# A two-layer encoder step in fp32: a third raw weight buffer in the second layer, and the third row tile loaded early into a query slot

## The chip, the cores and the metric

The kernel runs on one core of a Trainium2 chip. The time is the device time of one execution in microseconds, and lower is better. The median of several executions of the whole program counts.

## The reference

The reference is one inference step of a small encoder with two layers. There are 1024 prompt rows (one stream) and 128 sample rows (8 running streams with 16 new rows each), all of width 1024. Everything is float32.

```python
for layer in range(2):
    if layer == 0:    # mixer A: own q, k, v; window of 2 earlier chunks; ALiBi; sinks
        q, k, v = project_a(h, g_attn[0], w_qkv_a[0], g_q_a[0], g_k_a[0])
    else:             # mixer B: shared k, v from h; own q; 8 earlier chunks; learned bias
        k, v = shared_kv(h, g_kv, w_kv, g_k_b)
        q = project_q_b(h, g_attn[1], w_q_b[0], g_q_b[0])
    h = h + attention(q, k, v) @ w_o        # 16 heads of 64, 4 key/value heads, chunks of 64
    h = h + square(relu(rmsnorm(h, g_mlp[layer]) @ w_up[layer])) @ w_down[layer]   # 1024 -> 4096 -> 1024
```

Each `project` is an RMS norm over the 1024 columns, a matrix product, and an RMS norm of each head's 64 numbers for queries and keys. The sample rows also attend to cached keys and values. The outputs are the final rows of both kinds and the new keys and values of both mixers.

## The kernel before

**Tiles.** The prompt is cut into eight row tiles of 128 rows, numbered 0 to 7; the sample rows are one more tile, `ST`, number 8. A row tile of x (128 × 1024 numbers) is 512 KB. Between the phases the tiles live in DRAM, one tensor `xd[t]` for each.

**Exact products from three passes.** TensorE works on rounded float32. So each operand is split into a high part (the rounded number) and a low part (the rest), and a product is three matmuls, high × high, high × low and low × high: lines L198 to L200 for the projections, L157 to L159 for the output projection, L727 to L729 for the MLP. The high and low parts of a transposed x tile are called `hh` and `hl`.

**Weights.** A block of weights is loaded by SyncE into a raw buffer (`raw`, 512 KB for each load, from the pool `self.rawp`) and then split into its place in `w`. In the second layer GpSimd makes the high part (L166) and VectorE the low part (L171); each reads the raw buffer, which is free for another load when both have read it. `load_block` (L127) loads four such pieces for the keys and values (w_kv) and four for each half of the query weights (w_q_b). `load_wo` (L140) loads eight pieces of the output weights. The pool has two buffers, and the tag `raw` is also used for other things of the same size: an x tile in front of its transposes (`X`, L1331), the stacked sample keys `kt8` (L1401), the residual tile `xo` of an output projection inside the attention phase (L1510), and some x tiles of the output projection's last phase (L638).

**Phases.** Each layer runs `attention`, `wo_phase` (the rest of the output projection and the norm before the MLP), `mlp_up` and `mlp_down`. There are pools for each phase. Memory of a finished phase is taken again by the next, so that a new tile may have to wait until an old one at the same place has been read or stored. The program is recorded in an order written by hand, and a scheduler with a cost model then sets the order on each engine; each engine runs its instructions strictly in that order, and SyncE issues nearly all loads and stores in one such sequence.

**The second layer's attention.** First come the weights of keys and values and the tiles x0, x1 and `ST`. Then follow, for each tile, these steps:

- `X(t)`: loads `xd[t]`. Tile `ST` goes into a buffer of `biasB`; the others go into a `raw` buffer.
- `N(t)`: transposes x on TensorE (L191), splits the result into `hh` (ScalarE, L109) and `hl` (VectorE, L115), and takes the statistics of the norm (ScalarE, `junk`, L182). `spill` stores `hh` and `hl` to `hTd[t]` (L1361) for later, since two halves of the queries are made from them at different times.
- `K1(t)`, `K2(t)`: projection of keys and values, then norm and transposes into `KT`.
- `Q1(t, nb)`, `Q2(t, nb)`: projection of one half of the queries (8 heads), then norm, and transposes (L241) into a tile `qT`, of which the pool `apool` has two buffers.
- `R(t)`: loads `hh` and `hl` back from `hTd[t]` (L1374) for the second half of the queries. `hh` and `hl` have one buffer each.
- the scores (L412, L480), the softmax and its products, and the output projection of finished tiles (`WO`, with `xo` and a store to `xd`).

The text order at the place of the change, with `A` false, is: `load_block` of keys and values, X(0), X(1), X(ST), N(0), N(1), N(ST), small loads, the first half of the query weights, K1 and K2 and Q1 of tiles 0, 1 and ST, X(2), Q2(0), N(2), X(3), and so on.

**The last phase of the output projection.** `wo_phase` fetches nine tiles of x, apart from those kept in memory, into five places in turn: two of tag `raw` and three of its own pool `work` (L637 to L640).

Of the kernel before, what the change touches and what calls it, by code (L numbers as in the profile page):

```python
# [16 lines left out]
P = 128  # L17
# [58 lines left out]
class Build:  # L76
# [40 lines left out]
    def raw(self, shape):  # L117
        self.nraw += 1
        pool, tag = self.raws[self.nraw % len(self.raws)]
        return pool.tile(shape, F32, tag=tag, name=tag, bufs=2)  # L120

    def load_block(self, dst, w, n0, g, ks=range(0, KC, 2), act=False):
        nc = self.nc
# [500 lines left out]
    def wo_phase(self, layer, sx, x8, wo):  # L624
        nc = self.nc
        with ExitStack() as st:
            self.psum_pools(st, f"wo{layer}", dict(m=(4, 1), g=(3, 1)), dict(m="m", n="g"))
            work = self.pool(st, f"wow{layer}")
            small = self.pool(st, f"wosm{layer}", 2)
            osp, xs = {}, {}  # L630
            lo, hi = slice(0, 512), slice(512, 1024)

            def O(t, z):
                if t in self.kept:
                    xs[t] = self.kept[t]
                    return
                if len(xs) % 5 < 2:  # L637
                    xs[t] = self.rawp.tile([P, D], F32, tag="raw", name="x")  # L638
                else:
                    xs[t] = work.tile([P, D], F32, tag="x", name="x", bufs=3)  # L640
                nc.sync.dma_start(xs[t], self.xd[t])
                if t in self.wo_done:
                    return
                with self.tc.high_priority(WO_PRIO) if len(osp) < 2 else nullcontext():
                    load_o(t, z)

            def second():
                self.last = work.tile([P, 4, P], F32, tag="o2", name="o2")
                return self.last

            def load_o(t, z):
                o = work.tile([P, 4, P], F32, tag=f"o{z}", name="o")
                self.load_halves(layer, 1, t, o, second, nc.vector)
                oh = work.tile([P, 4, P], F32R, tag=f"oh{z}", name="oh")
                ol = work.tile([P, 4, P], F32R, tag=f"ol{z}", name="ol")
                self.split(oh, ol, o)
                osp[t] = oh, ol

            def M(t):
                x = xs[t]  # L660
                for n in range(2) if t not in self.wo_done else ():
                    nn = slice(n * 512, n * 512 + 512)
                    ps = self.psum("m", [P, 512], "ps_wo")
                    self.wo_proj(ps, *osp[t], wo, nn)
                    nc.vector.tensor_tensor(x[:, nn], ps, x[:, nn], ALU.add)
                if t not in self.wo_done:
                    nc.scalar.dma_start(self.xd[t], x)
                if t not in self.kept:
                    self.norm(small, work.tile([P, D], mybir.dt.bfloat16, tag="junk", name="junk"), x)

            def turn(src, dst, c, d):
                ps = self.psum("n", [P, 4, P], "ps_n")
                for k in range(4):
                    nc.tensor.transpose(ps[:, k, :], src[:, k * P : (k + 1) * P], self.ident)
                self.split(dst[0][:, d, c], dst[1][:, d, c], ps)

            def S(i):
                x1, x2 = xs[i], xs[i + NT // 2]
                s = self.sums() if i else self.sums0
                tt = nc.gpsimd.tensor_tensor  # L680
                tt(s[0], x2[:, lo], x2[:, hi], ALU.add)
                tt(s[1], s[0], x1[:, lo], ALU.subtract)
                tt(s[2], x1[:, lo], x2[:, lo], ALU.subtract)
                tt(s[3], x1[:, hi], s[1], ALU.subtract)
                return [x1[:, lo], x1[:, hi], x2[:, hi], *s]

            def T(i, src):
                c = slice(i * P, i * P + P)
                for p in (0, 1, 2, 3, 4, 5, 6):
                    turn(src[p], sx[p], c, slice(0, 4))  # L690

            order = WO_ORDER[layer]
            ready, pend = set(), []
            z = 0
            for t in order[:2]:
                O(t, z % 2)
                z += t not in self.wo_done
            for n, t in enumerate(order):
                if n + 2 < NTILE:
                    O(order[n + 2], z % 2)  # L700
                    z += order[n + 2] not in self.wo_done
                M(t)
                ready.add(t)
                for f in pend:
                    f()
                pend = []
                if t == ST:
                    def sample():
                        for h in range(2):
                            turn(xs[ST][:, h * 512 : h * 512 + 512], x8, slice(0, P), slice(4 * h, 4 * h + 4))  # L710
                    pend.append(sample)
                elif (t + 4) % NT in ready:
                    i = t % 4
                    T(i, S(i))
            for f in pend:
                f()
# [451 lines left out]
    def run(self):  # L1168
# [9 lines left out]
        with ExitStack() as top:  # L1178
# [49 lines left out]
            for layer in range(2):  # L1228
                with ExitStack() as st:
                    low = st.enter_context(ExitStack())  # L1230
                    self.rawp = self.pool(low, f"raw{layer}", 2)
                    self.wa = [self.pool(low, f"wa{layer}")]
                    self.nw = 0
                    keep = self.pool(low, f"keep{layer}")
# [39 lines left out]
    def attention(self, layer):  # L1274
# [18 lines left out]
        with ExitStack() as st:  # L1293
# [28 lines left out]
            def X(t):  # L1322
                if A:
                    xr[t] = work.tile([P, D], F32, tag="x", name="x", bufs=2)
                elif t == ST:
                    nb = cfg["bias_bufs"]
                    x = ring.tile([P, G, 256], F32, tag="biasB", name="x", bufs=nb)
                    xr[t] = x.rearrange("p g k -> p (g k)")
                else:
                    xr[t] = self.rawp.tile([P, D], F32, tag="raw", name="x")  # L1330
                nc.sync.dma_start(xr[t], x_src(t))  # L1331
# [218 lines left out]
                self.load_block(wkv, wkv_src, kv0, gkv, [4, 6])  # L1550
                N(ST, "p")
            else:
                if 0 in psp:
                    X(0)
                if 0 in psp:
                    for k0 in range(0, KC, 2):
                        self.load_split(wkv, 0, [k0, k0 + 1])
                        if k0 == 2:
                            X(1)
                else:  # L1560
                    self.load_block(wkv, wkv_src, kv0, gkv)
                    X(0)
                    X(1)
                X(ST)
                N(0)
                N(1, "pt")
                if not cfg["late"]:
# [43 lines left out]
            spill(ST)  # L1611
            run(Q1(ST, 0, "s"))
            K2(ST)
            X(2)
            Q2(0, 0)
            N(2)
            X(3)
# [118 lines left out]
def make_plan(tail, second):  # L1736
    plan = {}
    for s in range(2 * NT):
        if s + 2 < NT:
            plan[2 * s] = [("Q", s + 2)]  # L1740
        elif s + 2 < 2 * NT:
            plan[2 * s] = [("R", second[s + 2 - NT])]
        if s + 3 < NT:
            plan[2 * s + 1] = [("K", s + 3)]
    plan[13] = [("R", ST)]
    plan.update(tail)
    return plan
# [7 lines left out]
WO_ORDER = [[0, 4, 1, 5, 2, 6, 7, 3, ST], [0, 4, 1, 5, 6, 2, 7, 3, ST]]  # L1755

CFG = [
    dict(banks=dict(g=(5, 1), s=(2, 1), m=(1, 1)), q_bufs=4, order={}, second=SECOND[0], plan=make_plan({15: [('A', 0)], 17: [('A', 1)], 19: [('A', 2)], 21: [('A', 3)], 23: [('A', 4)], 25: [('A', 5)], 30: [('A', 7)], 31: [('A', 6)], 32: [('A', 8), ('B', 0), ('B', 4), ('B', 7)]}, SECOND[0]),
        la=3, prio=0, xt={('A', 8): 'x', ('B', 7): 'x', ('B', 0): 'keep', ('B', 4): 'keep'}, late=0, eng='cgu', k2=3, q2=9, lead=3, sf=0, up=(99, 2, 0, 3), ld=((9, 9, 10, 10), (11, 11, 12, 13), (26, 27, 28, 29)), n='g', q='g', qrb=1, np=3, bias_bufs=3, p_bufs=3, psp=(), wr='mmmm', wt=(0, 0, 2, 0, 2, 2, 0, 0, 2), rx=1, kd=1, o2=0, sb=0),
    dict(banks=dict(g=(4, 1), s=(3, 1), m=(1, 1)), q_bufs=4, order={}, second=SECOND[1], plan=make_plan({15: [('A', 0)], 17: [('A', 1)], 19: [('A', 2)], 21: [('A', 3)], 23: [('A', 4)], 25: [('A', 5)], 27: [('A', 8)], 28: [('A', 7)], 29: [('A', 6)], 31: [('B', 0), ('B', 4), ('B', 1)], 32: [('B', 5), ('B', 2), ('B', 3)]}, SECOND[1]),  # L1760
        la=2, prio=1000, xt={('B', 0): 'keep', ('B', 4): 'keep', ('B', 1): 'hh', ('B', 5): 'hl', ('B', 2): 'hh', ('B', 3): 'hl'}, late=0, eng='Ogu', k2=3, q2=6, lead=9, sf=0, up=(4, 2, 0, 99), ld=((11, 11, 11, 11), (11, 11, 11, 11), (26, 27, 28, 29)), n='g', q='g', qrb=2, np=2, bias_bufs=2, p_bufs=10, psp=(), wr='mmmm', wt=(0, 0, 0, 1, 1, 1, 1, 1, 2), rx=0, kd=1, o2=1, sb=3),
]

# [43 lines left out]
```

## Time and profile before

| | us |
|---|---|
| median of 3 runs | 2391.8 |
| lowest, highest | 2388.46, 2393.51 |
| the profiled execution | 2387.86 |
| its span | 2386.1 |

The profile is that of a single execution, whose time, 2387.86 us, is its span and 1.76 us around it. Its mean granted TensorE clock is 0.996 of full speed. Lines such as L191 are lines of the kernel before. PE is TensorE (PEld its weight loads), DVE VectorE, ACT ScalarE, POOL GpSimd, SP SyncE.

The second layer's attention begins at about 1140 us, where the first layer's MLP ends, and its output projection ends at about 1680 us.

### The profile page before, as it was taken

How to read it: one execution, taken by the hardware profiler on the slowest of the kernel's cores; microseconds unless marked ns; L12 is line 12 of the kernel's file. 1: busy time of each engine (PE TensorE's matmuls, PEld its weight loads, DVE VectorE, ACT ScalarE, POOL GpSimd, SP SyncE). 2: the span in 40 equal slices, each digit the busy share in tenths (PEclk: the TensorE clock that was granted, in tenths of full speed). 3: DMA queues.
4: the chain of work that ended last, by engine and by line, in shares of the span. 5: the costliest groups of instructions: out<-in, count | busy, mean ns of one | idle time of the engine just before them, and what ended most of it. 6: DMA issues, size and time to landing. Idle time of an engine off the chain costs nothing.

```text
span 2386.1 us, 33438 instructions
## 1 busy us (share of the span) xinstructions
PE 2313.9 (97%) x11621; PEld 1931.7 (81%) x11621; DVE 1627.6 (68%) x3002; ACT 1216.5 (51%) x2423; POOL 540.8 (23%) x828
## 2 busy tenths in 40 slices
PE   7998999899999999999999999998999999999999
PEld 6787877788888878888778788887888888888887
DVE  6788786655565776776577876877555565777674
ACT  3777674555555432332267666665555555323321
POOL 4334332311221100000333444444111211000000
PEclk9999999999999999999999999999999999999999
DMA  7335545343443964333653655554443445734332
GB/s 258 119 108 169 170 146 200 129 146 126 157 146 123 356 213 149 119 128 109 232 153 112 198 166 167 168 168 169 142 142 129 158 145 203 274 133 159 117 113 115
DMA packets 217529, 383.78 MB, mean 161 GB/s; under 512 B 50248, under 2 KB 124944, under 8 KB 210192
## 3 DMA queue, kind: packets, MB, share of 16 engines
q1 hardware_dynamic: 194288, 305.08, 38.9%
q0 software_dynamic: 21776, 71.84, 7.8%
q10 hardware_dynamic: 1296, 4.72, 0.5%
q8 instruction: 92, 1.51, 0.3%
q14 instruction: 77, 0.63, 0.1%
HBM read 245.42 MB, written 135.09 MB: 159 GB/s over the span
## 4 chain that ended last, share of the span: by engine, by line
PE 79%; DVE 7%; DMA 7%; ACT 3%; issue 2%; POOL 1%; SPq 1%; ACTq 0%; DVEq 0%; POOLq 0%
PE ps_x L727 9%; PE ps_x L729 9%; PE ps_x L728 9%; PE ps_y L729 7%; PE ps_y L728 7%; PE ps_y L727 7%; PE ps_mm L198 3%; PE ps_mm L200 3%; PE ps_mm L199 3%; PE ps_tr L305 2%; PE ps_mm L157 1%; PE ps_mm L158 1%; PE ps_mm L159 1%; PE ps_s L729 1%; PE ps_s L728 1%
## 5 line engine op out<-in xcount | busy, mean ns | idle before, releaser
L109 ACT CAST w<-r 128x2048 fp32r<-128x2048 f32 x56 | 107.1, 1913 | 325.2 <-PE ps_y L729 213.0
L727 PE MATMUL ps_x<-w,s 128*128 128x512 f32 x512 | 199.6, 390 | 4.2 <-DVE hc L866 2.1
L729 PE MATMUL ps_x<-w,s 128*128 128x512 f32 x512 | 199.4, 389 | 0.0
L728 PE MATMUL ps_x<-w,s 128*128 128x512 f32 x512 | 199.3, 389 | 0.0
L198 PE MATMUL ps_mm<-w,hh 128*128 128x512 f32 x432 | 172.5, 401 | 7.3 <-POOL w L166 3.2
L200 PE MATMUL ps_mm<-w,hl 128*128 128x512 f32 x432 | 172.1, 399 | 1.6 <-DVE hl L115 0.8
L199 PE MATMUL ps_mm<-w,hh 128*128 128x512 f32 x432 | 170.9, 397 | 1.3 <-DVE w L171 1.1
L109 ACT CAST s<-s 128x2048 fp32r<-128x2048 f32 x56 | 107.1, 1913 | 118.1 <-DMA s<-hd 109.3
L115 DVE TENSOR_TENSOR w<-r,w 128x2048 fp32r<-128x2048 f32 x56 | 128.2, 2290 | 51.0 <-ACT w L109 51.0
L727 PE MATMUL ps_x<-sx,w 128*128 128x512 f32 (+1 forms) x408 | 157.9, 387 | 3.9 <-ACT hc L846 3.0
L1033 DVE TENSOR_TENSOR x<-ps_y,x 128x512 f32<-128x512 f32 x136 | 92.4, 687 | 100.8 <-PE ps_y L729 100.8
L729 PE MATMUL ps_x<-sx,w 128*128 128x512 f32 (+1 forms) x408 | 154.2, 378 | 0.0
L728 PE MATMUL ps_x<-sx,w 128*128 128x512 f32 (+1 forms) x408 | 154.1, 378 | 0.0
L109 ACT CAST w<-ru 128x512 fp32r<-128x512 f32 (+1 forms) x160 | 110.0, 708 | 85.5 <-PE ps_y L728 32.0
L729 PE MATMUL ps_y<-w,s 128*128 128x512 f32 x384 | 149.5, 389 | 0.0
L727 PE MATMUL ps_y<-w,s 128*128 128x512 f32 x384 | 149.4, 389 | 0.0
L728 PE MATMUL ps_y<-w,s 128*128 128x512 f32 x384 | 149.4, 389 | 0.0
L115 DVE TENSOR_TENSOR s<-s 128x2048 fp32r<-128x2048 f32 x56 | 128.0, 2286 | 29.1 <-ACT s L109 28.9
L115 DVE TENSOR_TENSOR ptl<-ps_tr,pth 128x512 fp32r<-128x512 f32 x180 | 122.5, 685 | 24.1 <-ACT pth L109 17.8
L115 DVE TENSOR_TENSOR w<-ru,w 128x512 fp32r<-128x512 f32 (+1 forms) x160 | 126.5, 793 | 11.2 <-ACT w L109 11.1
L115 DVE TENSOR_TENSOR wq<-ru,wq 128x1024 fp32r<-128x1024 f32 x32 | 39.7, 1240 | 131.9 <-ACT wq L109 131.9
L109 ACT CAST pth<-ps_tr 128x512 fp32r<-128x512 f32 x180 | 104.9, 595 | 45.0 <-PE ps_tr L305 36.7
(280 smaller groups left out, 6579.7 us busy)
## 6 DMA issues: line engine op xcount, KB each, us to landing
s<-hd SPq DMA_DIRECT2D x56, 1024.0 KB, 4.7
ru<-in_w_up SPq DMA_DIRECT2D x64, 512.0 KB, 4.0
r<-in_w_down SPq DMA_DIRECT2D x32, 1024.0 KB, 5.8
hd<-hc POOLq DMA_DIRECT2D x128, 256.0 KB, 2.7
hd<-hs POOLq DMA_DIRECT2D x96, 256.0 KB, 2.5
x<-xd SPq DMA_DIRECT2D x41, 512.0 KB, 4.4
o<-oTd SPq DMA_DIRECT2D x52, 256.0 KB, 5.0
xd<-xo SPq DMA_DIRECT2D x18, 512.0 KB, 2.8
```

Of the source, the lines that this page charges most:

```text
L109: a = nc.scalar.copy(hi, src)
L115: return a, e.tensor_tensor(lo, src, hi.bitcast(F32), ALU.subtract)
L157: nc.tensor.matmul(ps, oh[:, k, :], w[:, 0, k, nn], start=(k == 0), stop=False)
L158: nc.tensor.matmul(ps, oh[:, k, :], w[:, 1, k, nn], start=False, stop=False)
L198: nc.tensor.matmul(ps, a, w[:, 0, k, :], start=(k == 0), stop=False)
L199: nc.tensor.matmul(ps, a, w[:, 1, k, :], start=False, stop=False)
L200: self.lp = nc.tensor.matmul(ps, b, w[:, 0, k, :], start=False, stop=(k == KC - 1))
L305: self.lp = nc.tensor.transpose(pt[:, i, :], get(i), self.ident)
L727: a = mm(ps, ah, bh, start=first, stop=False, skip_group_check=True)
L728: mm(ps, ah, bl, start=False, stop=False, skip_group_check=True)
L729: return a, mm(ps, al, bh, start=False, stop=last, skip_group_check=True)
L1033: tt(xs[t][:, N[n]], ps, xs[t][:, N[n]], ALU.add)
```

## The change

The raw pool has as many buffers as a new entry of the layer's settings says: `rb=2` for the first layer, as before, and `rb=3` for the second. In `wo_phase` of the second layer the five places are now three of tag `raw` and two of `work`. In the attention of the second layer X(2) moves from behind K2(ST) to behind X(ST), and its tile is a `qT` buffer of `apool` instead of a `raw` buffer. Branches on `psp`, which is empty for both layers, are removed at that place. In the built program the scheduler sets the order of all this; on SyncE X(2) then comes right after X(1).

```diff
     def raw(self, shape):
         self.nraw += 1
         pool, tag = self.raws[self.nraw % len(self.raws)]
-        return pool.tile(shape, F32, tag=tag, name=tag, bufs=2)
+        return pool.tile(shape, F32, tag=tag, name=tag, bufs=self.rb if tag == "raw" else 2)
...
-                if len(xs) % 5 < 2:
+                if len(xs) % 5 < self.rb:
                     xs[t] = self.rawp.tile([P, D], F32, tag="raw", name="x")
                 else:
-                    xs[t] = work.tile([P, D], F32, tag="x", name="x", bufs=3)
+                    xs[t] = work.tile([P, D], F32, tag="x", name="x", bufs=5 - self.rb)
...
-                    self.rawp = self.pool(low, f"raw{layer}", 2)
+                    self.rb = CFG[layer]["rb"]
+                    self.rawp = self.pool(low, f"raw{layer}", self.rb)
...
                     xr[t] = x.rearrange("p g k -> p (g k)")
+                elif t == 2:
+                    xr[t] = apool.tile([P, D], F32, tag="qT", name="x", bufs=2)
                 else:
                     xr[t] = self.rawp.tile([P, D], F32, tag="raw", name="x")
...
-                if 0 in psp:
-                    X(0)
-                if 0 in psp:
-                    for k0 in range(0, KC, 2):
-                        self.load_split(wkv, 0, [k0, k0 + 1])
-                        if k0 == 2:
-                            X(1)
-                else:
-                    self.load_block(wkv, wkv_src, kv0, gkv)
-                    X(0)
-                    X(1)
+                self.load_block(wkv, wkv_src, kv0, gkv)
+                X(0)
+                X(1)
                 X(ST)
+                X(2)
                 N(0)
                 N(1, "pt")
...
             K2(ST)
-            X(2)
+            if A:
+                X(2)
             Q2(0, 0)
             N(2)
             X(3)
...
-    dict(banks=dict(g=(5, 1), s=(2, 1), m=(1, 1)), ...
+    dict(rb=2, banks=dict(g=(5, 1), s=(2, 1), m=(1, 1)), ...
...
-    dict(banks=dict(g=(4, 1), s=(3, 1), m=(1, 1)), ...
+    dict(rb=3, banks=dict(g=(4, 1), s=(3, 1), m=(1, 1)), ...
```

More of the change, by code (lines that the diff above doesn't have):

```diff
@@ L1757 @@
 CFG = [
-    dict(banks=dict(g=(5, 1), s=(2, 1), m=(1, 1)), q_bufs=4, order={}, second=SECOND[0], plan=make_plan({15: [('A', 0)], 17: [('A', 1)], 19: [('A', 2)], 21: [('A', 3)], 23: [('A', 4)], 25: [('A', 5)], 30: [('A', 7)], 31: [('A', 6)], 32: [('A', 8), ('B', 0), ('B', 4), ('B', 7)]}, SECOND[0]),
+    dict(rb=2, banks=dict(g=(5, 1), s=(2, 1), m=(1, 1)), q_bufs=4, order={}, second=SECOND[0], plan=make_plan({15: [('A', 0)], 17: [('A', 1)], 19: [('A', 2)], 21: [('A', 3)], 23: [('A', 4)], 25: [('A', 5)], 30: [('A', 7)], 31: [('A', 6)], 32: [('A', 8), ('B', 0), ('B', 4), ('B', 7)]}, SECOND[0]),
         la=3, prio=0, xt={('A', 8): 'x', ('B', 7): 'x', ('B', 0): 'keep', ('B', 4): 'keep'}, late=0, eng='cgu', k2=3, q2=9, lead=3, sf=0, up=(99, 2, 0, 3), ld=((9, 9, 10, 10), (11, 11, 12, 13), (26, 27, 28, 29)), n='g', q='g', qrb=1, np=3, bias_bufs=3, p_bufs=3, psp=(), wr='mmmm', wt=(0, 0, 2, 0, 2, 2, 0, 0, 2), rx=1, kd=1, o2=0, sb=0),
-    dict(banks=dict(g=(4, 1), s=(3, 1), m=(1, 1)), q_bufs=4, order={}, second=SECOND[1], plan=make_plan({15: [('A', 0)], 17: [('A', 1)], 19: [('A', 2)], 21: [('A', 3)], 23: [('A', 4)], 25: [('A', 5)], 27: [('A', 8)], 28: [('A', 7)], 29: [('A', 6)], 31: [('B', 0), ('B', 4), ('B', 1)], 32: [('B', 5), ('B', 2), ('B', 3)]}, SECOND[1]),
+    dict(rb=3, banks=dict(g=(4, 1), s=(3, 1), m=(1, 1)), q_bufs=4, order={}, second=SECOND[1], plan=make_plan({15: [('A', 0)], 17: [('A', 1)], 19: [('A', 2)], 21: [('A', 3)], 23: [('A', 4)], 25: [('A', 5)], 27: [('A', 8)], 28: [('A', 7)], 29: [('A', 6)], 31: [('B', 0), ('B', 4), ('B', 1)], 32: [('B', 5), ('B', 2), ('B', 3)]}, SECOND[1]),
         la=2, prio=1000, xt={('B', 0): 'keep', ('B', 4): 'keep', ('B', 1): 'hh', ('B', 5): 'hl', ('B', 2): 'hh', ('B', 3): 'hl'}, late=0, eng='Ogu', k2=3, q2=6, lead=9, sf=0, up=(4, 2, 0, 99), ld=((11, 11, 11, 11), (11, 11, 11, 11), (26, 27, 28, 29)), n='g', q='g', qrb=2, np=2, bias_bufs=2, p_bufs=10, psp=(), wr='mmmm', wt=(0, 0, 0, 1, 1, 1, 1, 1, 2), rx=0, kd=1, o2=1, sb=3),
```

## The prediction

> **What bounds the kernel now.** I read the page's first table, then the windows by stretch, then the waits of TensorE and SyncE between 1140 and 1700 us, and last the chain and the timelines around the few waits that the change can touch.
>
> ```profile
> PE 2313.9 (97%) x11621; PEld 1931.7 (81%) x11621; DVE 1627.6 (68%) x3002; ACT 1216.5 (51%) x2423; POOL 540.8 (23%) x828
> ...
> 1140.00:1200.00 60.00, 54.32 (x258) 45.03 (x257) 36.45 (x76) 18.72 (x40) 20.48 (x24) 0.97 0.67 228
> 1200.00:1600.00 400.00, 387.24 (x2132) 321.11 (x2131) 307.40 (x866) 268.03 (x749) 167.26 (x231) 1.00 0.53 162
> 1600.00:1700.00 100.00, 88.73 (x547) 76.05 (x546) 73.60 (x129) 60.74 (x132) 38.21 (x40) 0.97 0.41 139
> 1700.00:2386.00 686.00, 680.64 (x3182) 569.27 (x3180) 427.37 (x469) 285.62 (x351) 67.90 (x125) 1.00 0.44 155
> ```
>
> The columns after the stretch's length are busy us of PE, PEld, DVE, ACT and POOL, then the granted clock, the DMA share and GB/s. TensorE is busy 97% of the span, so only its idle time can be won. The last stretch (the second layer's MLP) has 5.4 us of it in 686. The second layer's attention and output projection have the rest: 60.00 − 54.32 = 5.7 us at the hand-over from the first layer's MLP, 12.8 us in 1200 to 1600, 11.3 us in 1600 to 1700. Compared instruction by instruction, the two programs hold the same work, and their orders differ only between about 1140 and 1680 us. So nothing outside these three rows can move, and at most some 30 us can be won.
>
> ```profile
> PE ps_n L191 <- DMA x<-xd: 4.9, 2, 2.9
> ...
> PE ps_mm L198 <- DMA hh<-hTd: 1.3, 1, 1.3
> ...
> PE ps_mm L200 <- DMA hl<-hTd: 0.6, 1, 0.6
> ```
>
> These are TensorE's waits (total us, times, longest). Two of them, 4.9 us together, are for an x tile's load; those loads are what the change touches.
>
> ```profile
> 1148.40 3.93 DMA x<-xd
> ...
> 1159.56 10.06 DMA xd<-x
> ...
> 1173.69 6.15 DMA raw<-in_w_q_b
> ...
> 1192.16 3.50 DMA x<-xd
> ...
> 1334.91 4.14 DMA hh<-hTd
> ```
>
> In the chain that ended last (start, us, what), the loads at 1148.40 and 1192.16 are x of row tiles 1 and 2.
>
> **Part 1, X(1) earlier.** With two raw buffers, SyncE (in order) issues a load only when the split of the one two before has ended, and X(0), X(1) take raw slots too.
>
> ```profile
> 1135.89 1.38 POOL L166 TENSOR_SCALAR w<-raw,gcol 128x512 fp32r<-128x512 f32 x2 [330.78 <-DMA raw<-in_w_kv]
> 1137.72 1.89 POOL L166 TENSOR_SCALAR w<-raw,gcol 128x512 fp32r<-128x512 f32 x2 [0.46 <-DMA raw<-in_w_kv]
> ...
> 1140.67 0.74 DVE L171 SCALAR_TENSOR_TENSOR w<-raw,gcol,w 128x512 fp32r<-128x512 f32 x1
> ...
> 1143.05 1.84 DVE L171 SCALAR_TENSOR_TENSOR w<-raw,gcol,w 128x512 fp32r<-128x512 f32 x2 [1.03 <-POOL w L166]
> ...
> 1147.64 0.73 DVE L171 SCALAR_TENSOR_TENSOR w<-raw,gcol,w 128x512 fp32r<-128x512 f32 x1
> ...
> 1148.63 1.03 PE L191 MATMUL ps_n<-identr,x 128*128 128x128 f32 x8
> 1149.42 0.48 PE L729 MATMUL ps_x<-w,s 128*128 128x512 f32 x1
> ...
> 1152.37 1.09 PE L191 MATMUL ps_n<-identr,x 128*128 128x128 f32 x8 [2.01 <-DMA x<-xd]
> ```
>
> X(1) is issued at 1148.40, when the fourth K/V block's split ends (1147.64 + 0.73), lands 3.93 later, and TensorE idles 2.01 us. With three buffers it waits for the third block's split instead. That block is loaded with the first two; two such loads arrived 1137.72 − 1135.89 = 1.83 us apart, so the third is there at 1139.55, its POOL half (1.38) ends at 1140.9, and its two L171 (1.84, with an L1033 between) follow the second block's, over at 1141.41: about 1143.3. X(1) then lands at about 1147.0. In the new order TensorE comes to N(0) after 17 matmuls of the MLP's product, not 29; at 0.2265 us each (1148.40 to 1148.63 is one) that is 1145.9, and x0's eight transposes take 0.79 (1148.63 to 1149.42), so it wants x1 at 1146.7. About 0.3 of the 2.01 us stay: **−1.7**, bounds −2.0 and −1.2 (a landing 0.5 us late).
>
> **Part 2, the sample tile's split.**
>
> ```profile
> 1170.72 1.17 DVE L171 SCALAR_TENSOR_TENSOR w<-raw,gcol,w 128x512 fp32r<-128x512 f32 x1 [4.45 <-POOL w L166]
> ...
> 1172.14 0.67 DVE L115 TENSOR_TENSOR hl<-ps_n,hh 128x512 fp32r<-128x512 f32 x1
> ...
> 1172.87 0.50 PE L200 MATMUL ps_mm<-w,hl 128*128 128x512 f32 x1 [0.79 <-DVE hl L115]
> ```
>
> VectorE idles 4.45 us in front of a weight split that waits, and the sample tile's hl, ready to run, stands behind it. In the new order both hl come ahead of that split. The gap of 1172.87 to its neighbour is 0.95 over the normal spacing: **−0.95**, bounds −0.95 and 0.
>
> **Part 3, X(2) early.** Its issue moves from 1192.16 to behind X(1), so it lands some 40 us before N(2); a qT slot, free until the first Q2, holds it. Behind it on SyncE stands the first query-weight load, which waits for the fourth K/V split (1148.37) anyway, so X(2)'s own issue costs nothing there; its 512 KB go out while no other weight is wanted.
>
> ```profile
> 1192.32 0.60 PE L241 MATMUL ps_q<-identr,qr 128*128 128x128 f32 x4
> 1195.80 1.47 PE L191 MATMUL ps_n<-identr,x 128*128 128x128 f32 x8 [2.88 <-DMA x<-xd]
> 1196.92 1.52 PE L412 MATMUL ps_sn<-KT,qT 128*128 128x128 f32 x6
> ...
> 1192.36 0.60 ACT L207 ACTIVATE qn<-ps_mm 128x512 f32<-128x512 f32 x1 [1.61 <-PE ps_mm L200]
> ...
> 1195.75 1.06 ACT L182 ACTIVATE junk<-x 128x1024 bf16<-128x1024 f32 x1 [0.62 <-DMA x<-xd]
> ...
> 1195.02 0.69 DVE L115 TENSOR_TENSOR qT<-ps_q,qT 64x512 fp32r<-64x512 f32 x1
> ```
>
> The 2.88 us are not all won. The scores (L412) need qT, which was ready at 1195.02 + 0.69 = 1195.71 behind ScalarE's queue, and with x2 there ScalarE now runs its statistics (junk, 1.06) in front of that queue. I put the first scores about 1 us earlier than 1196.92 on the same clock, and two projection matmuls (2 × 0.2265) now stand ahead of them: **−1.45**, bounds 0 (junk delays qT by all of it) and −2.88.
>
> **The clock.**
>
> ```profile
> 1196.00:1197.00 1.00, 1.00 (x9) 1.00 (x7) 0.23 (x2) 0.98 (x3) 0.71 (x1) 0.66 0.00 0
> 1197.00:1198.00 1.00, 1.00 (x7) 1.00 (x6) 0.93 (x4) 0.97 (x2) 0.55 (x1) 0.50 0.73 262
> 1198.00:1199.00 1.00, 1.00 (x8) 1.00 (x7) 0.97 (x2) 0.60 (x2) 0.00 (x0) 0.50 0.67 131
> 1199.00:1200.00 1.00, 1.00 (x6) 0.86 (x5) 0.97 (x3) 0.58 (x1) 0.00 (x0) 0.64 0.81 315
> ```
>
> Behind the pause at 1195.80 the granted clock is half: (0.34 + 0.50 + 0.50 + 0.36) / 0.5 = 3.4 us of it, so at most 1.7 us lost; behind the 2.01 us pause at 1152.37 the eight transposes take 1.09 instead of 1.47, so no drop. The new pause by part 3 is about 2.3 us (from 1192.92, with transposes and two matmuls in it): between the two. I take half, **−0.9**, bounds −1.7 and 0. The Trainium skill ("TensorE: Matmul & The Clock Gate", Part 1: The HAM clock gate) says that the clock halves after at least one idle window of about 3.4 us, and that a busy one restores it; the half-clock time agrees, the pause of 2.88 us is shorter than the page's window. By its rule alone a pause of 2.3 us is safe and the term would be −1.7.
>
> **Part 4, what is pushed back.** The second and third query-weight loads are now free to issue ahead of the store of tile 7 (at 1159.56 before), and the store took 10.06 us to land under a DMA share of 0.67. The first split of the query weights waits for that store, because its buffer lies over x7.
>
> ```profile
> 1169.99 3.13 POOL L166 TENSOR_SCALAR w<-raw,gcol 128x512 fp32r<-128x512 f32 x4 [4.62 <-DMA hTd<-hl]
> ...
> 1179.92 3.39 POOL L166 TENSOR_SCALAR w<-raw,gcol 128x512 fp32r<-128x512 f32 x4 [0.69 <-DMA raw<-in_w_q_b]
> ```
>
> Two loads of 1.83 us in front cost the store up to 3.7, less the 1.7 by which all comes earlier: the split starts between 1168.3 and 1172, and TensorE wants its first product at about 1170.2 (1172.87 − 0.95 − 1.7). In return the third block no longer waits for a split (1173.69, 6.15 us to land), but the fourth does. Loss **+0.5**, bounds 0 and +2.
>
> **Part 5, the rest.** After N(2) every weight, x and xo load that takes a raw slot stands one tile earlier in the instruction order; kt8 and the eight w_o loads share the pool. No wait for raw is among TensorE's, so I take 0, with ±4 for the reshuffled order out of the 12.8 us. In the output projection x has three raw slots and two of its own instead of two and three: five in turn as before, 0 ± 1.5. The removed psp branches ran nowhere: 0.
>
> Sum: −1.7 − 0.95 − 1.45 − 0.9 + 0.5 = **−4.5 us**. The profiled execution took 2387.86 us (span 2386.1), 3.9 below the median; it becomes 2383.4, and the median 2391.8 becomes **2387.3**. Parts 1 to 4 at their ends give −7.5 to +0.8.
>
> **Rivals.** B, a larger gain: earlier loads also shorten the small waits of 1200 to 1600 (1.3 and 0.6 for hTd among them). Half of that row's 12.8 us idle: −4.5 − 6.4 = −10.9, 2380.9. For it: each of those loads has one tile more of time. Against: most of that idle is on VectorE and ScalarE chains.
>
> C, no change: the query-weight split or qT takes the place of the waits removed. TensorE then stands at the second pause as long as before and part 4 costs its 2: about 2391.8. Against: POOL has only 3.13 us of work there.
>
> D, slower: the hh and hl of tiles loaded back (L1374) now have one more 512 KB load in front of them.
>
> ```profile
> 1330.76 0.90 SPq L127 DMA_DIRECT2D raw<-in_w_q_b  x2
> 1334.91 0.34 SPq L1374 DMA_DIRECT2D hh<-hTd  x1
> ...
> L1374 SPq DMA_DIRECT2D hh<-hTd x9: 320/338/538, 1334.9 to 1491.8; - x9
> ```
>
> hh and hl have one buffer each, so their loads can't go earlier, and the first one is already 1.3 us late. In the new order three raw loads, not two, stand just before it, and an xo load moves ahead of later ones. If six of the nine pairs land 1.83 us later with no slack, that is +11.0, net **+6.5**, 2398.3; it decides from about three pairs on (+5.5 against −4.5). Against: a third load that was free earlier may have landed by then. The Trainium skill ("DMA: Bandwidth & Descriptors", Issuing engines are not separate DMA queues) has all transfers on the same 16 engines whoever issues them, which speaks for D; the 10.06 us store in the busy stretch agrees. At its 436 GB/s a 512 KB load takes an estimated 1.2 us, and six pairs would cost 7.2.
>
> **How the numbers follow.** Forecast 0.44, B 0.20, C 0.11, D 0.25. About 0.2% (4.8 us) is what a measurement of this kernel can tell from no change. The forecast lies just inside it, so a little under half of its chance is beyond: faster 0.21 + 0.20 = 0.41, same 0.23 + 0.11 = 0.34, slower 0.25. The forecast's own range is 2384.3 to 2392.6. The range given goes beyond B's and D's centres by about 1 us, 2379.5 to 2399.5, and leaves less than half of D and of B out, some 0.18.
>
> **What would show it.** Right: the pair of transposes of N(0) and N(1) without a pause near 1146; no pause before the sample tile's L200; N(2) straight behind L241, then 2 us idle with qT as its releaser, and a clock that stays at 1.00; the 1140 to 1200 stretch some 4 us shorter, the later ones alike. Wrong: a wait of L198 for the L166 or L171 of the query weights near 1170, or hh<-hTd waits that grow in number (D), or a 1200 to 1600 stretch that changes by more than 4 us.

## The result: slower by 0.26%, and the profile after

| | before | changed |
|---|---|---|
| median of 22 runs, us | 2388.59 | 2395.38 |
| lowest, highest | 2383.78, 2395.57 | 2388.60, 2400.28 |
| ratio of the times | | 1.0026 (95%: 1.0019 to 1.0033) |
| profiled execution, us | 2387.86 | 2394.38 |
| its span, us | 2386.1 | 2392.6 |

The changed kernel is slower by 6.8 us, while 4.5 us of gain were forecast. The windows of the changed kernel, by the stretches of the prediction (length; busy us of PE, PEld, DVE, ACT, POOL; granted clock; DMA share; GB/s), and a few shorter ones:

```profile
1140.00:1200.00 60.00, 56.29 (x270) 45.80 (x269) 37.97 (x76) 19.60 (x42) 22.91 (x27) 1.00 0.73 246
...
1300.00:1400.00 100.00, 89.29 (x483) 71.39 (x482) 80.14 (x211) 67.90 (x188) 43.65 (x52) 0.98 0.50 156
1400.00:1600.00 200.00, 199.25 (x1107) 166.62 (x1106) 154.90 (x430) 131.26 (x369) 84.74 (x120) 1.00 0.54 167
```

The hand-over (first row) gained: TensorE is busy 56.29 us instead of 54.32, and the clock is 1.00 instead of 0.97 (in this trace; a second one, below, has a drop there). From 1300 to 1400 us TensorE idles 10.7 us. In the kernel before that row reads

```profile
1300.00:1400.00 100.00, 95.35 (x524) 77.36 (x523) 86.11 (x226) 71.68 (x197) 45.25 (x54) 1.00 0.54 164
1400.00:1600.00 200.00, 195.65 (x1086) 164.34 (x1085) 149.34 (x413) 125.78 (x356) 84.70 (x118) 1.00 0.55 174
```

so 4.7 us. The changed kernel gets 3.6 us back in 1400 to 1600. TensorE's waits between 1140 and 1700 us in the changed kernel:

```profile
PE ps_n L674 <- DVE sx L115: 8.5, 4, 4.8
PE ps_mm L198 <- DMA hh<-hTd: 3.3, 1, 3.3
PE ps_tr L305 <- POOL p L462: 2.0, 2, 1.1
PE ps_mm L198 <- ACT hh L109: 1.9, 1, 1.9
```

The x loads' 4.9 us are gone from the top. The wait for hh<-hTd has grown from 1.3 to 3.3 us, a wait for GpSimd's p is new, and that of the last phase for sx has grown from 6.1 to 8.5.

Since fixed windows hold other work in each kernel, I also lined the traces up by work: each TensorE instruction counts with its usual spacing in the kernel before, and the table says how much later each kernel reaches the same sum of work, stretch by stretch (us; stretches by the first trace of before; sums of rounded parts).

| trace | to 1140 | 1140-1200 | 1200-1265 | 1265-1330 | 1330-1365 | 1365-1640 | 1640-1690 |
|---|---|---|---|---|---|---|---|
| before, second trace | -2.8 | -0.6 | -2.9 | +2.1 | -0.1 | 0.0 | -0.3 |
| changed | +1.6 | -2.9 | +0.4 | +1.5 | +8.3 | -5.3 | +2.9 |
| changed, second trace | +1.1 | -3.0 | +1.6 | +0.7 | +7.8 | -4.4 | +3.1 |
| X(2) early alone | +1.1 | -1.8 | +6.3 | +1.8 | 0.0 | +1.2 | -0.2 |
| X(2) early, scores first | -0.6 | -1.3 | +1.8 | +1.1 | -0.1 | +0.3 | -0.1 |
| third buffer alone | +3.6 | -2.1 | -0.6 | +0.5 | +8.5 | -3.5 | +2.1 |
| changed, third buffer only at the hand-over | +4.1 | -2.9 | +1.1 | +2.5 | -0.2 | +3.1 | +0.3 |
| changed, w_o load held | +0.8 | -2.1 | +3.1 | +1.4 | +6.8 | -2.0 | +1.6 |
| changed, xo loads held | +2.8 | -2.2 | +1.5 | +1.3 | +8.4 | -2.2 | +2.1 |
| changed, both held | +1.2 | -3.4 | +0.1 | +2.5 | +5.4 | -2.8 | -0.7 |
| third buffer alone, both held | -2.8 | -2.6 | -1.8 | +0.8 | +5.2 | -4.5 | -0.1 |

The first column is work in which the orders do not differ, so it shows how far single executions stray: 7 us from lowest to highest. Times are therefore judged by medians; the table says where.

### The profile page after: what moved, and what is told of

It reads as the page before. It is cut to its first block, busy times and chain, and to the rows that moved or that the text cites. A ratio compares the mean times of both kernels' runs of the same rounds, so it can differ in the third digit from the quotient of the medians.

```text
span 2392.6 us, 33429 instructions
## 1 busy us (share of the span) xinstructions
PE 2319.7 (97%) x11621; PEld 1934.4 (81%) x11621; DVE 1628.6 (68%) x3002; ACT 1216.5 (51%) x2423; POOL 541.9 (23%) x828
## 4 chain that ended last, share of the span: by engine, by line
PE 79%; DMA 7%; DVE 6%; ACT 3%; issue 2%; POOL 1%; SPq 1%; ACTq 0%; DVEq 0%; POOLq 0%
PE ps_x L727 9%; PE ps_x L729 9%; PE ps_x L728 9%; PE ps_y L729 7%; PE ps_y L728 7%; PE ps_y L727 7%; PE ps_mm L198 3%; PE ps_mm L200 3%; PE ps_mm L199 3%; PE ps_tr L305 2%; PE ps_mm L157 2%; PE ps_mm L159 1%; PE ps_mm L158 1%; PE ps_s L729 1%; PE ps_s L728 1%
## 5 line engine op out<-in xcount | busy, mean ns | idle before, releaser
L198 PE MATMUL ps_mm<-w,hh 128*128 128x512 f32 x432 | 174.8, 406 | 11.8 <-POOL w L166 3.4
L200 PE MATMUL ps_mm<-w,hl 128*128 128x512 f32 x432 | 173.1, 401 | 0.5 <-DMA hl<-hTd 0.3
```

The lines of the kernel that those rows point to most:

```text
L198: nc.tensor.matmul(ps, a, w[:, 0, k, :], start=(k == 0), stop=False)
L200: self.lp = nc.tensor.matmul(ps, b, w[:, 0, k, :], start=False, stop=(k == KC - 1))
```

## The experiments

**The parts one by one.** The changed kernel with `rb=2`, and the changed kernel without the lines of X(2):

```diff
-    dict(rb=3, banks=dict(g=(4, 1), ...
+    dict(rb=2, banks=dict(g=(4, 1), ...
```

> Two raw buffers as before; only X(2) is early, in a qT slot. From the reload of tile 0 on, SyncE's order is that of the kernel before. Theory Q (the loss is the third 512 KB load ahead of the hh and hl reload near 1335 us and what follows from it): faster than before by 1 to 3 us, since the pause ahead of N(2) shrinks and the clock stays up, and no loss near 1340. Theory O (the loss comes from the whole reshuffled order of the attention and the output projection, whichever load is moved): slower than before by 2 to 5 us, since the order between 1200 and 1680 changes here too.

```diff
-                elif t == 2:
-                    xr[t] = apool.tile([P, D], F32, tag="qT", name="x", bufs=2)
...
-                X(2)
                 N(0)
...
-            if A:
-                X(2)
+            X(2)
```

> Three raw buffers, X(2) at its old place in a raw slot. SyncE's order from the reload of tile 0 on is that of the changed kernel: three weight loads just ahead of hh. Theory Q: as slow as the changed kernel or slower by up to 3 us (the pause at N(2) is back), 6 to 10 us slower than before, with hh landing some 3 us later than before near 1340. Theory O: anything from 0 to 8 us slower; the pause near 1340 may be there without setting the time.

X(2) alone: 1.0013 (1.0004 to 1.0022), median 2394.07 against 2390.26. The third buffer alone: 1.0032 (1.0020 to 1.0045), 2398.40. So neither part is a gain, and theory Q failed for X(2): it forecast a gain there. The two do not add up to the whole either (1.0026). The table says where each loses: X(2) between 1200 and 1265 us, the third buffer between 1330 and 1365 us.

**A third buffer for the hand-over alone**, first with the other qT buffer in its place, then with x of tile 3 keeping the third raw buffer to the end:

```diff
-            raw = self.raw([P, 2, 512])
+            raw = other() if other and k0 == 4 else self.raw([P, 2, 512])   # other: a qT buffer; rb=2
```

> Two raw buffers; the third piece of the key and value weights goes into the second qT buffer and X(2) into the first, so that the hand-over has its third buffer and the rest of the phase has none. The fourth weight piece comes later in SyncE's order than in the changed kernel. Theory Q: faster than before by 1 to 4 us, no loss near 1340. Theory O: slower than before by 2 to 5 us.

```diff
+                if t == 3:
+                    self.held = xr[t]
...
+            if not A:      # behind the last addition of the attention phase
+                self.behind(self.late_add, nc.vector.memset(self.held[:, :1], 0.0))
             run(work_of(32))
```

> The changed kernel, but x of tile 3 keeps its raw buffer to the end of the attention phase, by an empty write behind the last addition there. So the hand-over has three buffers and the early X(2), and from about 1200 us on two buffers are left; the order of every engine's TensorE work from about 1270 us on is that of the kernel before. Theory L (the loss lies behind 1300 us, where the third buffer lets 512 KB loads and their splits run ahead of the reloads and of the softmax): 1 to 4 us faster than before. Theory H (the loss lies in the hand-over and the scores right behind it, 1190 to 1260 us, as X(2) alone seemed to show): 2 to 5 us slower than before.

The first: 1.0008 (0.9999 to 1.0018), between the forecasts of theories Q and O, which tells little; its trace, lined up in the same way, has −0.1 us in 1330 to 1365. The second: 1.0000 (0.9991 to 1.0009), 2390.15 against 2389.82. With the third buffer gone from about 1200 us on, the 6.8 us of loss are gone; the loss of 1330 to 1365 us is −0.2 in the table. Theory H is out, and of theory L the place holds, but not the gain of 1 to 4 us: in the trace, what the hand-over wins (2.9) is lost again before 1330 (1.1 and 2.5). That trace is of an execution 5.8 us above its kernel's median.

**What stands ahead of the reloads.** In the changed kernel SyncE, TensorE and the clock near the first reload (start, us, instruction; then one-microsecond windows):

```profile
1331.58 0.39 SPq L127 DMA_DIRECT2D raw<-in_w_q_b  x1
1332.07 2.82 SPq L140 DMA_DIRECT2D raw<-in_w_o_b  x2
1335.53 0.33 SPq L1377 DMA_DIRECT2D hh<-hTd  x1
```

```profile
1342.48 0.71 PE L198 MATMUL ps_mm<-w,hh 128*128 128x512 f32 x1 [3.33 <-DMA hh<-hTd]
```

```profile
1342.00:1343.00 1.00, 0.52 (x2) 0.44 (x2) 1.00 (x3) 0.80 (x3) 1.00 (x1) 0.77 0.99 399
1343.00:1344.00 1.00, 0.93 (x3) 0.33 (x2) 1.00 (x3) 0.00 (x0) 0.53 (x1) 0.50 1.06 375
1344.00:1345.00 1.00, 1.00 (x3) 0.81 (x3) 1.00 (x4) 0.00 (x0) 0.00 (x0) 0.50 0.97 284
1345.00:1346.00 1.00, 1.00 (x4) 0.72 (x4) 1.00 (x3) 0.66 (x1) 0.00 (x0) 0.52 0.96 296
```

The third load ahead of hh is an output-weight load that two buffers would not have let out yet. TensorE waits for hh until 1342.48 (before: until 1339.19), and 0.23 + 0.50 + 0.50 + 0.48 = 1.7 us of clock go with it. From the issue of hh to TensorE's start it is 6.95 us instead of 4.28. The second trace of the changed kernel has the same three loads in front, but the wait there is

```profile
1340.66 0.76 PE L198 MATMUL ps_mm<-w,hh 128*128 128x512 f32 x1 [1.42 <-DMA hh<-hTd]
```

which is about what it was before. In that trace the clock is low from 1339.9 on, for 6.8 us, 3.4 us of clock, and the stretch of 1330 to 1365 us loses 7.8 us all the same. So the loss of this stretch came twice, and its division between wait and clock did not. The early blocks' splits also run ahead of the softmax, on VectorE and on GpSimd. The reciprocal (L459) that the tile's p waits for, in the changed kernel and then in the kernel before:

```profile
1332.52 0.75 DVE L171 SCALAR_TENSOR_TENSOR w<-raw,gcol,w 128x512 fp32r<-128x512 f32 x1
1333.18 0.69 DVE L115 TENSOR_TENSOR ptl<-ps_tr,pth 128x512 fp32r<-128x512 f32 x1
1333.79 0.74 DVE L171 SCALAR_TENSOR_TENSOR w<-raw,gcol,w 128x512 fp32r<-128x512 f32 x1
...
1335.17 0.16 DVE L459 RECIPROCAL li<-l 128x2 f32<-128x2 f32 x1
```

```profile
1332.94 0.16 DVE L459 RECIPROCAL li<-l 128x2 f32<-128x2 f32 x1
```

It is 2.2 us later. VectorE was 0.9 us late before the first of the two L171, and each of these puts what follows it off by 0.65 us. GpSimd then runs a split in front of p too, in the changed kernel (first) as against the kernel before:

```profile
1335.19 1.36 POOL L166 TENSOR_SCALAR w<-raw,gcol 128x512 fp32r<-128x512 f32 x2 [6.57 <-DMA raw<-in_w_q_b]
1336.53 2.13 POOL L462 TENSOR_SCALAR p<-p,li 128x640 f32<-128x640 f32 x2
```

```profile
1333.28 1.59 POOL L462 TENSOR_SCALAR p<-p,li 128x640 f32<-128x640 f32 x2 [6.23 <-DVE li L459]
```

So p starts 3.25 us later: 2.2 by the reciprocal, and the rest behind that L166. Three kernels order loads behind reloads (`behind` sets an order on SyncE, no wait):

```diff
+            if self.rb == 3 and half == 0 and k == 1:      # in load_wo
+                self.behind(self.r_first, ld)              # reload of tile 0
```

> The changed kernel, in which the second output-weight load is ordered behind the reload of tile 0 (hh and hl), so that two 512 KB loads stand just ahead of it as before, not three. Theory Q: hh lands some 3 us sooner, the half clock near 1343 is gone, and the time falls by 3 to 6 us against the changed kernel, to within 3 us of before. Theory O: the time stays within 2 us of the changed kernel.

```diff
+                if not A and not half and t in (0, 1):     # xo loads, in WO
+                    self.behind(self.r_st, ld)             # reload of tile ST
+                if not A and not half and t == 2:
+                    self.behind(self.r_second, ld)         # reload of tile 1
```

This second edit alone:

> The changed kernel with only the xo loads of tiles 0, 1 and 2 ordered behind the reloads of the sample tile and of tile 1; the second output-weight load still stands ahead of the reload of tile 0. With the kernels that hold only the output-weight load (no gain) and both (the whole loss gone) it makes a square. If the xo loads ahead of the reloads are the cause: within 2 us of before, and TensorE's loss in the output projection near 1660 us gone. If both are needed, each by itself hiding behind the other: 4 us or more slower than before.

Both edits:

> The changed kernel with the second output-weight load ordered behind the reload of tile 0, and the xo loads of tiles 0 and 1 behind the reload of the sample tile, that of tile 2 behind the reload of tile 1: no reload has more 512 KB loads just ahead of it than before. The third buffer still lets the weight splits run early on VectorE and GpSimd. If the transfers ahead of the reloads are the loss (theory Q, in its wider form), the time is within 2 us of before. If the splits ahead of the softmax are (theory S), the stall of L305 on GpSimd's p (L462) near 1341 us stays and the time is 4 us or more above before.

The weight load alone: 1.0028 (1.0017 to 1.0040), no gain. The xo loads alone: 1.0041 (1.0027 to 1.0055). Both: 1.0000 (0.9991 to 1.0009), 2390.83 against 2389.82. So the loss is gone when these loads are held behind the reloads, and both groups have to be. Why one is not enough is seen in the trace with only the weight load held:

```profile
1349.10 1.45 SPq L1520 DMA_DIRECT2D xo<-xd  x2
1352.55 0.38 SPq L525 DMA_DIRECT2D vc<-in_cache_v_b  x1
1353.20 0.32 SPq L1379 DMA_DIRECT2D hh<-hTd  x1
```

```profile
PE ps_mm L200 <- DMA hh<-hTd: 2.7, 1, 2.7
PE ps_tr L307 <- POOL p L464: 1.8, 2, 1.0
```

The first reload no longer makes TensorE wait, but the freed buffers take two xo loads ahead of the second reload, and the same pause stands there (lines of this kernel are 2 or more higher: L200 is the L198 of before). With both held, the waits of 1330 to 1365 us are

```profile
PE ps_tr L307 <- POOL p L464: 1.8, 2, 1.0
PE ps_mm L200 <- DMA hh<-hTd: 1.8, 1, 1.8
PE ps_mm L202 <- DMA hl<-hTd: 0.6, 1, 0.6
```

The wait for p is still there (in this stretch it was 0.9 us in the first trace of the changed kernel and 1.1 in the second), so the splits ahead of the softmax were not taken away: theory S holds for the stall, though not for its price. Of the 8.3 us in that stretch 5.4 stay, later stretches give 2.8 and 0.7 back, and the median is that of before.

The table also shows where the repair of the changed kernel lies, and it is mostly not at the reloads. From 1330 to 1640 us the changed kernel loses 8.3 − 5.3 = 3.0 us net, with both groups held 5.4 − 2.8 = 2.6. From 1640 to 1690 us it is +2.9 against −0.7. With the third buffer alone it is the other way round: 5.0 against 0.7, then +2.1 against −0.1. So holding the loads removes the loss; that it does so by letting hh and hl land sooner is shown for part of it only. Why TensorE regains 2 to 5 us between 1365 and 1640 us is open as well.

The last phase went along. In the changed kernel VectorE there has

```profile
1651.48 1.29 DVE L622 SCALAR_TENSOR_TENSOR x<-x,mrs,gb 128x1024 f32<-128x1024 f32 x1 [2.60 <-DMA xd<-x]
```

in front of the splits that TensorE waits for: it overwrites x, whose store to `xd` must land first. The scheduler chose this order in the four programs with three buffers throughout in which the second w_o load may go ahead (the changed kernel, the third buffer alone, the xo loads held, and the scores first with no load held). The wait is 2.3 to 4.0 us there, and the first three lose 2.1 to 3.1 us in the table's last column. Holding the w_o load alone is enough to be rid of the order, but not of the whole loss (1.0028). With both groups held the stretch 1640 to 1690 is −0.7 instead of +2.9. That the same repair moves both is shown; how the one order leads to the other is not.

**Where X(2)'s gain goes.** The first scores of the changed kernel, then of X(2) alone:

```profile
1193.84 1.04 PE L191 MATMUL ps_n<-identr,x 128*128 128x128 f32 x8
1196.83 0.50 PE L198 MATMUL ps_mm<-w,hh 128*128 128x512 f32 x1 [1.95 <-ACT hh L109]
...
1197.41 0.78 PE L412 MATMUL ps_sn<-KT,qT 128*128 128x128 f32 x6
```

```profile
1198.14 0.78 PE L412 MATMUL ps_sn<-KT,qT 128*128 128x128 f32 x6
...
1204.61 0.86 PE L412 MATMUL ps_sn<-KT,qT 128*128 128x128 f32 x6
...
1215.32 0.74 PE L412 MATMUL ps_sn<-KT,qT 128*128 128x256 f32 x4 [0.65 <-ACT p L452]
```

N(2) follows L241 without a pause, and what is left, 1.95 us, did not lower the clock in this trace (the row of 1140 to 1200 has 1.00). That was luck. The second trace of the same kernel has, behind the same pause,

```profile
1195.56 0.50 PE L198 MATMUL ps_mm<-w,hh 128*128 128x512 f32 x1 [1.95 <-ACT hh L109]
```

```profile
1196.00:1197.00 1.00, 1.00 (x9) 0.95 (x8) 1.00 (x3) 0.97 (x2) 0.20 (x1) 0.77 0.98 389
1197.00:1198.00 1.00, 1.00 (x6) 1.00 (x6) 0.97 (x3) 0.97 (x3) 0.00 (x0) 0.50 1.02 383
```

and 0.50 and 0.53 after that, 1.7 us of clock. Also, hh of tile 2 is there before qT, so the scheduler lets all of tile 2's projection (22 matmuls) go ahead of the second six scores. These are through at 1205 instead of 1201, the softmax starts so much later, and near 1215 TensorE waits for it with no projection left to fill in: it idles 1.9 us between 1214 and 1218, and then the clock is 0.75, 0.50, 0.50 and 0.54, 1.7 us more. The changed kernel has the same projection ahead of its second scores (at 1203.51), but no drop of the clock there, and loses only 0.4 and 1.6 us in this stretch in its two traces. The edit that puts the first group's scores ahead:

```diff
+            if self.gate is not None and k == 1:      # second chunk of tile 2's K1
+                self.behind(self.gate, first)         # the first group's last score
```

> Two raw buffers, only X(2) early, and tile 2's key and value projection after its first chunk is ordered behind the first group's scores, so that the first scores come ahead of the projection on TensorE, as in the kernel before. The kernel with X(2) alone was 3 us slower than before, by 6 us lost between 1200 and 1265 us in its trace. Theory F (with x2 there early, the projection is put ahead of the scores, the softmax starts later, and its matmuls are missing as filler near 1215 us): the loss of 1200 to 1265 us shrinks by 3 us or more, and the time is from 3 us faster than before to equal. Theory T (the load's transfer itself, 512 KB in the busy hand-over, costs it): as slow as with X(2) alone, 2 to 4 us slower than before.

It gave 0.9988 (0.9979 to 0.9997), 2389.15 against 2391.12, where X(2) alone had 1.0013: theory F. The second four scores are at

```profile
1199.14 1.11 PE L414 MATMUL ps_sn<-KT,qT 128*128 128x128 f32 x4
```

This is the one version measured faster than both kernels, by 0.12%. That it is faster than X(2) alone is clear, since the two intervals do not meet. That it is faster than the kernel before is less so: its interval ends at 0.9997, and it is one of fourteen versions.

**Combinations.**

> Three raw buffers at the hand-over only (x of tile 3 keeps its buffer to the end of the attention phase), X(2) at its old place. Theory F: the gain of the third buffer at the hand-over stays, without the loss behind N(2) and without the loss behind 1330 us: 1 to 3 us faster than before, and faster than the same with X(2) early by as much. Theory T: the same, since no early X(2) is there. If neither holds, within 1 us of before.

> Three raw buffers throughout, X(2) at its old place, and the loads that ran ahead of the reloads of tiles 0, ST and 1 ordered behind them. Theory Q in its wider form: the loss of 8 us of three buffers alone is gone, and the time is within 2 us of before, or up to 3 us faster. If the splits ahead of the softmax count as much as the transfers, 3 us or more slower than before.

> Three raw buffers at the hand-over only, X(2) early, and the first scores ahead of tile 2's projection. Theory F: 2 to 5 us faster than before, the best of all, since both gains of the hand-over stay and neither loss is there. Theory T: within 2 us of before, as without the new order.

> The changed kernel with the first group's scores ordered ahead of tile 2's projection after its first chunk; the loads ahead of the reloads are left as in the changed kernel. If the two causes add up (the scores behind the projection at 1200 to 1240 us, the loads ahead of the reloads from 1330 us on), it is 1 to 3 us faster than the changed kernel and still 3 us or more slower than before, with the loss of 1330 to 1365 us in full (7 to 9 us). If the later loss follows from the earlier one, it is gone too and the time is within 2 us of before.

> The changed kernel with both repairs: the first scores ahead of tile 2's projection, and the three groups of loads behind the reloads. If the two causes add up: 1 to 4 us faster than before and than either repair alone. If something else of the change still costs time, within 2 us of before.

| third buffer | X(2) | scores first | loads held | ratio (95%) | median against before |
|---|---|---|---|---|---|
| hand-over | late | no | | 0.9996 (0.9983 to 1.0010) | 2390.92, 2391.12 |
| throughout | late | no | both | 0.9991 (0.9978 to 1.0004) | 2388.29, 2391.12 |
| hand-over | early | yes | | 0.9999 (0.9988 to 1.0010) | 2391.52, 2391.12 |
| throughout | early | yes | no | 1.0042 (1.0029 to 1.0055) | 2399.67, 2389.95 |
| throughout | early | yes | both | 0.9999 (0.9990 to 1.0008) | 2389.90, 2389.95 |

With three buffers the order of the scores gains nothing, with the loads held or not: theory F's forecast of 2 to 5 us failed there, and the two causes are not a sum. Holding the loads is worth 0.4% with the scores first (1.0042 to 0.9999) and 0.26% without. No version with a third buffer is measurably faster than before.

**How far two traces of one program differ.** The kernel before and the changed one once more:

> The kernel before once more, for a second trace of it: how far two profiled executions of one program differ, stretch by stretch. All theories: under 1 us in each of the stretches 1140 to 1200, 1200 to 1330, 1330 to 1400, 1400 to 1650 and 1650 to 1690 us, unless the arrival of transfers makes them differ by more.

> The changed kernel once more, for a second trace. Theories L and S: again a loss of 5 us or more between 1330 and 1400 us. Theory H: a loss between 1200 and 1260 us that the first trace did not show.

They took 2383.33 and 2395.38 us. The forecast of under 1 us in each stretch was wrong for the kernel before, which strays by 2 to 3 us between 1200 and 1330 us; the +8, the −5 and the +3 of the changed kernel came again.

The clock has a part in the difference. The 22 executions of the changed kernel have a mean granted clock of 0.9937, and the sets of executions of the kernel before that were timed beside the other versions 0.9947 to 0.9952. My estimate from this is 0.0010 to 0.0015 of 2390 us, 2.4 to 3.6 us of the 6.8. Within the changed kernel, the five executions at 0.996 took 2388.60 to 2391.08 us and the seven at 0.992 took 2393.08 to 2400.28.

## Why the prediction was wrong

**Part 1, −1.7: right in kind, too large.** N(1) still waits.

```profile
1142.56 2.49 SPq L1334 DMA_DIRECT2D x<-xd  x3
...
1149.45 1.09 PE L191 MATMUL ps_n<-identr,x 128*128 128x128 f32 x8 [0.93 <-DMA x<-xd]
```

0.93 us remain of 2.01, so 1.1 are won. (The prediction's own 1143.3 and 3.93 give a landing at 1147.2, not 1147.0, and so 0.5 us left, not 0.3.) The three x loads now go out within 2.5 us, and TensorE starts on x1 at 1149.45. Of the 2.4 us behind the forecast 1147.0, 1.6 is the lag that this execution had by 1140 us. The rest fits X(2) right behind X(1), a transfer that the prediction took for free: with the third buffer alone, where that load is not there, 0.3 us remain.

**Part 2, −0.95: right.** No wait of L200 for hl is left at the sample tile.

**Part 3 and the clock, −1.45 and −0.9: right at the place, and lost again behind it.** The stretch around N(2), 1190 to 1200 us, gained about 2 us in both traces. The clock stayed up in the first and fell in the second, so taking half for it was reasonable, and "a clock that stays at 1.00" held in one trace of two. The pause left is 1.95 us, as forecast, but it ends on hh and not on qT. A step failed here too: I named the chain to the first scores and not what TensorE would do meanwhile. With X(2) alone the projection that fills the pause is missing later, and the second scores wait behind it. In the changed kernel that loss is not clear, and putting the scores first gained nothing there.

**Part 4, +0.5: right in size by luck, since it came at another place.** The split did not make TensorE wait near 1170; GpSimd's high part cost half a microsecond at

```profile
1181.16 0.50 PE L198 MATMUL ps_mm<-w,hh 128*128 128x512 f32 x1 [0.49 <-POOL w L166]
```

Together the hand-over won 2.9 us in the first trace and 3.0 in the second, of 4.5.

**Part 5, 0 with ±4: the step that failed.** "No wait for raw is among TensorE's, so I take 0" asked what the third buffer would free, not what it would let out ahead of others. What it let out, w_o and xo loads ahead of the reloads and their splits ahead of the softmax, cost 8 us between 1330 and 1365; 5 came back by 1640. The output projection, for which the prediction had 0 ± 1.5 since five places stay five, cost 3 more, through an order that has VectorE wait for a store. It is not the places: the kernel with the third buffer only at the hand-over has the same five and loses 0.3 us there. With the loads held the kernel as a whole is at 1.0000, so even then the 3 us of the hand-over do not show in its time.

**Rival D** named the place and the sign; its net +6.5 is near the measured +6.8 by luck, and not by its sum. Not six reloads were 1.83 us later each for TensorE: in the first trace only the wait for the first one grew, by 2 us, with 1.7 of clock and the softmax's own delay, and in the second trace not even that one. Some 3 us of this stay by 1640, and the other 3 are in the last phase, which D did not name. D's point of decision, three pairs, was wrong as well. The Trainium skill ("DMA: Bandwidth & Descriptors", Issuing engines are not separate DMA queues) has transfers interleave on the same 16 engines; the first hl took

```profile
1335.94 7.69 DMA hl<-hTd
```

and that of the next tile in the kernel before, by its chain of waits,

```profile
1346.25 5.07 DMA hl<-hTd
```

which fits, though these are two different tiles. The chances had 0.25 on slower. The low weight came from reading the rest of the phase by its waits for what the change adds, none, instead of by its waits with no slack at all: the reload was already 1.3 us late.

## What to carry to other kernels

A further buffer in a shared pool is also permission for loads to run ahead: look in the new order of the issuing queue for what now stands in front of each load that can't be early, and price that load first. When a wait of the main engine is removed, ask which filler work it will spend there, and whether the chain that was fed from that work's place comes later for it. If a load can be brought in early, pin the order of what it unlocks; here, with two buffers, that turned 0.13% slower into 0.12% faster, and with three it gained nothing. Take a second trace before a drop of the clock, or its absence, is put down to the change.

## What the runs showed of the hardware

The length of a single pause did not decide whether TensorE's clock halved. Near N(2) it fell behind 2.88 us (before), behind 1.62 us (X(2) early, scores first), and not behind 2.46 us (third buffer alone, both held). Behind the same 1.95 us in the same program it stayed at 1.00 in one execution and fell in the next (changed). What decides is open; near N(2) TensorE ran only transposes just before the pause, just behind it, or both, so the stretch without other matmuls was longer than the pause. When it fell it was low for 3.4 us, the 1.7 us of lost clock above, and in three traces for 6.8 us (in the changed kernel's second from 1339.9). Two executions of one program differed by up to 3 us within a stretch of 65 us.
